# Decoder step on one core: the samples' last store goes out on SyncE instead of GpSimd, and VectorE evicts its rows

## The chip, the cores and the metric

The kernel runs on one core of a Trainium2 chip, as one launch. The metric is the device time of that launch in microseconds. Engines are named as the profile names them: PE (TensorE matmuls), DVE (VectorE), ACT (ScalarE), POOL (GpSimd), SP (SyncE). SP, ACT and POOL can issue DMAs.

## The reference

One step of a hybrid decoder trunk of one layer, for 256 prompt tokens and 8 sample tokens that share the weights (width 2048, f32):

```
h = RMSNorm(x);  q|k|v|z|xBC|dt|qm|gates = h @ w_in
A = sliding-window attention;  B = Mamba-2 SSD;  M = cross-attention into 256 memory tokens
x = x + (sig(gA)*(A @ w_up_swa) + sig(gB)*(B @ w_up_ssd) + sig(gM)*(M @ w_up_mem)) @ w_out
x = x + (silu(h2 @ w_gate) * (h2 @ w_up)) @ w_down        # h2 = RMSNorm(x), d_ff 5632
```

It returns `y_prompt` (1, 256, 2048), `y_sample` (8, 1, 2048) and the new caches and states. What the change touches is the very last piece of the last line: columns 1536 to 2047 of `y_sample`.

## The kernel before

**Layout.** Activations stand transposed: features on the 128 partitions, the 264 tokens (256 prompt, then 8 samples) along the free axis. Each projection is cut into groups of 512 output features, four PSUM tiles of 128 x 264. Weights come in `raw` tiles of 512 KB on SP's queue (L261), are split into a rounded high part (`hi`, ACT, L181) and a rest (`lo`, DVE, L182), and each weight block gives three matmuls (L160).

**The last product.** The FFN runs in three passes over d_ff; in each, `down(i, ...)` for i = 0 to 3 adds 512 features of `@ w_down` to `x2["x"]` in SBUF. In the third pass the sums are outputs. For i = 0 to 2, `y_out` turns tiles by a DVE transpose and stores them from POOL (L1764: a 16 KB store of the samples; L1767: four 128 KB stores of the prompt). For i = 3, `group` is given `bank=y_bank`: it finishes the four PSUM tiles one after the other (c = 0 to 3) and calls `y_bank(ps, c)` after each.

**`y_bank`.** For every c, DVE adds the residual: 8 sample columns (L1777) into `yo_s`, 256 prompt columns (L1779) into `yo`, for c = 3 in two halves. For c = 0 to 2, DVE turns the prompt's columns in 32 x 32 blocks into the buffer `ring` (L1782), and four stores of 32 KB go out, two on SP and two on ACT (L1785). For c = 3 PE turns instead: first `yo_s`, which holds the samples' columns of all four c, into 32 rows of 128 (L1789, written `tr`, shown by the profile as L164, tile `yt`), then the two halves of the prompt's last 128 features. The samples' rows are copied to `ring` and stored (L1790, L1791: 16 KB); the two prompt halves are copied by DVE (t = 0) and ACT (t = 1) and stored by SP and ACT (L1799, L1797, L1800: 64 KB each).

**Order.** A scheduler places each engine's instructions; the order in which the code is written sets their priority. `keep_in_program_order` pins the transposes. Each engine works through its own list in order and waits on semaphores. When the kernel function returns, closing code follows that the profile puts on L1913: each engine's queue is drained, SP waits for the semaphores of the outstanding DMAs, and POOL gathers all engines in a barrier, clears the semaphores and releases them.

Of the kernel before, what the change touches and what calls it, by code (L numbers as in the profile page):

```python
# [12 lines left out]
AF = mybir.ActivationFunctionType  # L13
# [5 lines left out]
P = 128  # L19
# [58 lines left out]
def tile_hybrid_decoder_step(  # L78
# [9 lines left out]
    nc = tc.nc  # L88
    act = nc.scalar.activation
    V = nc.vector  # L90
# [18 lines left out]
    def t4(name, dt=F32):  # L109
        return tp.tile([P, 4 * NT], dt, tag="t4", name=nm(name), bufs=4)  # L110
# [45 lines left out]
    def sps(name):  # L156
        return pq.tile([P, 512], F32, tag="s", name=nm(name))
# [4 lines left out]
    def tr(out, in_):  # L162
        n = in_.shape[0]
        return nc.tensor.transpose(out, in_, ident[0:n, 0:n])  # L164
# [1606 lines left out]
    def y_bank(ps, c):  # L1771

        if c == 0:
            y_end["o"] = t4("yo")
        yo, yo_s = y_end["o"][:, 0:4 * NP].rearrange("p (c n) -> p c n", c=4), y_end["o"][:, 4 * NP:4 * NT]
        x = x2["x"](12 + c)
        V.tensor_tensor(yo_s[:, c * NS:(c + 1) * NS], ps[c][:, NP:NT], x[:, NP:NT], op=ALU.add)  # L1777
        for cols in (slice(0, NP),) if c < 3 else (slice(0, P), slice(P, NP)):
            V.tensor_tensor(yo[:, c, cols], ps[c][:, cols], x[:, cols], op=ALU.add)  # L1779
        if c < 3:  # L1780
            ot = ring[:, c * NP:(c + 1) * NP]
            V.transpose(ot, yo[:, c, 0:NP])  # L1782
            to = y_prompt[0].rearrange("(j t) (k a f) -> k a t j f", t=32, a=4, f=32)[12 + c]
            for a in range(4):
                (nc.sync, nc.scalar)[a % 2].dma_start(to[a], ot[32 * a:32 * a + 32].rearrange("p (j f) -> p j f", f=32))  # L1785
            return
        rows = ring[0:32, 2048 - P:2048]
        ts = sps("yt")
        tc.keep_in_program_order(tr(ts[0:32, 0:P], yo_s))  # L1789
        act(rows, ts[0:32, 0:P], AF.Copy)  # L1790
        nc.gpsimd.dma_start(y_sample.rearrange("b s (k f) -> k (b s) f", f=P)[12:16], rows)  # L1791
        for t in range(2):
            turned = (dps, sps)[t]("yt")
            tc.keep_in_program_order(tr(turned[:, 0:P], yo[:, 3, t * P:(t + 1) * P]))
            ot = ring[:, 1024 + (2 + t) * P:1024 + (3 + t) * P]
            if t:
                act(ot, turned[:, 0:P], AF.Copy)  # L1797
            else:
                V.tensor_copy(ot, turned[:, 0:P])  # L1799
            (nc.scalar if t else nc.sync).dma_start(y_prompt[0, t * P:(t + 1) * P, 15 * P:16 * P], ot)  # L1800
# [116 lines left out]
```

## Time and profile before

| | us |
|---|---|
| median of three runs (1865.42, 1865.45, 1867.88) | 1865.45 |
| the profiled execution, whole | 1866.6 |
| its span, first to last instruction | 1864.9 |
| PE busy in it | 1852.9 |
| DVE / ACT / POOL busy | 1201.3 / 956.2 / 149.6 |

The span lies inside the profiled execution's own time; 1.7 us lie around it. The profile is of one execution, the median of others, so a sum is made against 1866.6 and 1864.9 and then set beside 1865.45. "L1791" is line 1791 of the kernel. "POOLq" or "SPq" are an engine's queue (DMA issues, waits, drains), which are not counted as busy. Instructions of the closing code stand on L1913, those of the opening code on L1904.

### The profile page before, as it was taken

What the parts mean: (1) busy time and instruction counts of PE and PEld (TensorE: products, weight loads), DVE (VectorE), ACT (ScalarE), POOL (GpSimd) and SP (SyncE); (2) the same over time, 40 slices, a digit from 0 to 9 for tenths busy, and PEclk for the clock granted to TensorE, in tenths of its full rate; (3) what the DMA queues carried; (4) which work ended last, traced back from release to release, by engine and by line L of the source; (5) the groups of instructions that cost most, each with busy time, mean ns of one, the idle gap of its engine ahead of it and who ended that gap; (6) DMA issues with size and microseconds to landing.
All of it is one profiled execution on the core that took longest, in us unless ns stands there. A gap on an engine that the chain in (4) does not pass through costs nothing.

```text
span 1864.9 us, 37297 instructions
## 1 busy us (share of the span) xinstructions
PE 1852.9 (99%) x15094; PEld 1811.8 (97%) x15094; DVE 1201.3 (64%) x2329; ACT 956.2 (51%) x1413; POOL 149.6 (8%) x299
## 2 busy tenths in 40 slices
PE   9999999999999999999999999999999999999998
PEld 7899999998999999999999999999999999999998
DVE  6766578776788878887465675555445555445564
ACT  6745466665777676764444444443334443334442
POOL 1010002101111111120000001000000000100001
PEclk9999999999999999999999999999999999999999
DMA  9786669677777777787878766556765556865565
GB/s 308 241 253 213 203 226 303 212 242 237 239 229 263 239 240 245 245 258 236 230 230 252 183 202 213 183 185 179 183 186 183 183 186 185 232 199 181 182 198 132
DMA packets 209669, 406.36 MB, mean 218 GB/s; under 512 B 29319, under 2 KB 34422, under 8 KB 209488
## 3 DMA queue, kind: packets, MB, share of 16 engines
q1 hardware_dynamic: 181552, 324.62, 57.9%
q0 software_dynamic: 21776, 74.10, 11.9%
q10 hardware_dynamic: 6168, 5.25, 0.9%
q8 instruction: 118, 1.93, 0.4%
q14 instruction: 55, 0.45, 0.1%
HBM read 378.38 MB, written 27.81 MB: 218 GB/s over the span
## 4 chain that ended last, share of the span: by engine, by line
PE 60%; issue 1%; DVE 0%; POOL 0%; POOLq 0%; DVEq 0%
PE pg L160 14%; PE pu L160 14%; PE pdn L160 13%; PE pin L160 7%; PE pout L160 5%; PE pus L160 5%; PE pua L160 2%; DVE lo L182 0%; PE py L160 0%; POOL out_dram L1767 0%; PE pst L160 0%; DVE ring L1763 0%; DVE ring L1504 0%; DVE y L1463 0%; DVE xp L1761 0%
## 5 line engine op out<-in xcount | busy, mean ns | idle before, releaser
L182 DVE TENSOR_TENSOR lo<-raw,hi 128x1024 fp32r<-128x1024 f32 (+1 forms) x651 | 746.9, 1152 | 547.8 <-ACT hi L181 545.5
L181 ACT ACTIVATE hi<-raw 128x1024 fp32r<-128x1024 f32 (+1 forms) x651 | 647.6, 1002 | 815.0 <-PE pin L160 188.8
L160 PE MATMUL pin<-hl,hi 128*128 128x264 f32 x1728 | 486.1, 284 | 0.0
L160 PE MATMUL pin<-hh,hi 128*128 128x264 f32 x1728 | 485.5, 284 | 0.0
L160 PE MATMUL pin<-hh,lo 128*128 128x264 f32 x1728 | 474.6, 283 | 0.1
L160 PEld LDWEIGHTS pin<-hl,hi 128*128 128x128 f32 x1728 | 324.2, 188 | 3.7 <-issue 3.6
L160 PEld LDWEIGHTS pin<-hh,hi 128*128 128x128 f32 x1728 | 323.8, 188 | 3.9 <-issue 3.4
L160 PEld LDWEIGHTS pin<-hh,lo 128*128 128x128 f32 x1728 | 318.2, 188 | 3.7 <-issue 3.1
L160 PE MATMUL pu<-h2l,hi 128*128 128x264 f32 x704 | 197.8, 282 | 0.0
L160 PE MATMUL pu<-h2h,hi 128*128 128x264 f32 x704 | 197.7, 282 | 0.0
L160 PE MATMUL pdn<-fal,hi 128*128 128x264 f32 x704 | 197.7, 282 | 0.0
L160 PE MATMUL pg<-h2l,hi 128*128 128x264 f32 x704 | 197.7, 283 | 0.0
L160 PE MATMUL pdn<-fah,hi 128*128 128x264 f32 x704 | 197.3, 282 | 0.0
L160 PE MATMUL pg<-h2h,hi 128*128 128x264 f32 x704 | 197.0, 282 | 0.0
L160 PE MATMUL pdn<-fah,lo 128*128 128x264 f32 x704 | 194.8, 282 | 0.0
L160 PE MATMUL pu<-h2h,lo 128*128 128x264 f32 x704 | 194.7, 282 | 0.0
L160 PE MATMUL pg<-h2h,lo 128*128 128x264 f32 x704 | 194.4, 282 | 0.0
L160 PEld LDWEIGHTS pdn<-fal,hi 128*128 128x128 f32 x704 | 132.0, 188 | 0.0
L160 PEld LDWEIGHTS pg<-h2l,hi 128*128 128x128 f32 x704 | 132.0, 187 | 0.0
L160 PEld LDWEIGHTS pu<-h2l,hi 128*128 128x128 f32 x704 | 132.0, 187 | 0.0
L160 PEld LDWEIGHTS pg<-h2h,hi 128*128 128x128 f32 x704 | 132.0, 187 | 0.0
L160 PEld LDWEIGHTS pu<-h2h,hi 128*128 128x128 f32 x704 | 131.9, 187 | 0.0
(530 smaller groups left out, 2935.3 us busy)
## 6 DMA issues: line engine op xcount, KB each, us to landing
raw<-in_w_in_dram SPq DMA_DIRECT2D x216, 512.0 KB, 4.5
raw<-in_w_gate_dram SPq DMA_DIRECT2D x88, 512.0 KB, 3.6
raw<-in_w_up_dram SPq DMA_DIRECT2D x88, 512.0 KB, 3.9
raw<-in_w_down_dram SPq DMA_DIRECT2D x88, 512.0 KB, 5.0
raw<-in_w_up_ssd_dram SPq DMA_DIRECT2D x32, 512.0 KB, 6.0
raw<-in_w_out_dram SPq DMA_DIRECT2D x32, 512.0 KB, 5.1
raw<-in_w_mem_kv_dram SPq DMA_DIRECT2D x31, 512.0 KB, 5.2
ring<-in_state_ssm_dram POOLq DMA_DIRECT2D x32, 256.0 KB, 5.0
```

The lines of the kernel that those rows point to most:

```text
L160: return nc.tensor.matmul(out, lhsT=lhsT, rhs=rhs, start=start, stop=stop)
L181: h = act(hi, src, AF.Copy)
L182: return h, V.tensor_tensor(lo, src, hi.bitcast(F32), op=ALU.subtract)
```

## The change

The copy of the samples' rows out of PSUM is a DVE `tensor_copy` instead of an ACT activation, and the store is issued on SP's queue instead of POOL's. The rows, their place in `ring` and the destination are the same.

```
         rows = ring[0:32, 2048 - P:2048]
         ts = sps("yt")
         tc.keep_in_program_order(tr(ts[0:32, 0:P], yo_s))
-        act(rows, ts[0:32, 0:P], AF.Copy)
-        nc.gpsimd.dma_start(y_sample.rearrange("b s (k f) -> k (b s) f", f=P)[12:16], rows)
+        V.tensor_copy(rows, ts[0:32, 0:P])
+        nc.sync.dma_start(y_sample.rearrange("b s (k f) -> k (b s) f", f=P)[12:16], rows)
```

Where it puts the two instructions, at the end of three engines' lists (line, operation, output<-input, shape). On DVE, behind the residual adds of c = 3:

```order
 L1777 TENSOR_TENSOR yo_22122<-pdn_22003,x_1710_12828 128x8
 L1779 TENSOR_TENSOR yo_22122<-pdn_22003,x_1710_12828 128x128 x2
+L1790 COPY ring<-yt_22183 32x128
 L1799 COPY ring<-yt_22187 128x128
 L1913 UNCONDITIONAL_BRANCH
```

The copy stands between the last add and the copy of the first prompt half. On SP's queue, behind the last weight load and the six stores of c = 0 to 2:

```order
 L261 DMA raw_22028<-in_w_down_dram 128x2x512
 L1785 DMA out_dram<-ring 32x8x32 x6
+L1791 DMA out_dram<-ring 4x8x128
 L1800 DMA out_dram<-ring 128x128
 L1913 UNCONDITIONAL_BRANCH
```

The samples' store now stands ahead of SP's own last store. On POOL, the end of the list:

```order
 L1764 DMA out_dram<-ys_21982 16x8x32
 L1767 DMA out_dram<-ring 32x8x128 x4
-L1791 DMA out_dram<-ring 4x8x128
 L1913 UNCONDITIONAL_BRANCH
 L1913 ISA
```

POOL's last own work is now the store of the prompt's features of i = 2. On ACT the copy of L1790 is gone from between the six stores of L1785 and the copy of L1797; PE's list is the same.

## The prediction

> **What bounds the kernel now.** The head of the page, read first, says where 99% of the time is.
>
> ```profile
> span 1864.9 us, 37297 instructions
> PE 1852.9 (99%) x15094; PEld 1811.8 (97%) x15094; DVE 1201.3 (64%) x2329; ACT 956.2 (51%) x1413; POOL 149.6 (8%) x299
> ```
>
> PE is busy from end to end; nothing in the change touches a matmul that lies ahead of the last store, so the body of the program stays as it is. All that can move lies behind the last projection matmul. The second view is therefore the chain that ended last, from 1835 us on; its last five pieces are:
>
> ```profile
> 1841.82 1.39 POOL out_dram L1767 x3
> 1843.21 0.33 issue
> 1843.54 0.58 POOL out_dram L1767
> 1844.12 14.28 issue
> 1858.40 0.63 POOLq L1913
> ```
>
> The chain ends on POOL's own queue, in the closing code (L1913), not on PE, SP or ACT. The 14.28 us of "issue" are POOL waiting for the sample's rows. The third view, the timeline from 1852 us on without the weight loads, shows what is done there; columns are start, duration, engine, line, operation.
>
> ```profile
> 1853.67 3.71 SPq L1785 DMA_DIRECT2D out_dram<-ring  x6
> 1853.67 3.78 ACTq L1785 DMA_DIRECT2D out_dram<-ring  x6
> ...
> 1856.70 0.28 PE L160 MATMUL pdn<-fah,lo 128*128 128x264 f32 x1
> 1857.10 0.48 DVE L1779 TENSOR_TENSOR yo<-pdn,x 128x128 f32<-128x128 f32 x2
> 1857.24 0.73 PE L164 MATMUL yt<-ident,yo 128*32 128x128 f32 x3 [0.26 <-DVE yo L1777]
> 1857.81 0.29 DVE L1799 COPY ring<-yt 128x128 f32<-128x128 f32 x1 [0.23 <-PE yt L164]
> 1857.87 0.27 ACT L1790 ACTIVATE ring<-yt 32x128 f32<-32x128 f32 x1 [8.59 <-PE yt L164]
> 1858.04 0.27 ACT L1797 ACTIVATE ring<-yt 128x128 f32<-128x128 f32 x1
> 1858.13 0.36 SPq L1800 DMA_DIRECT2D out_dram<-ring  x1
> 1858.34 0.37 ACTq L1800 DMA_DIRECT2D out_dram<-ring  x1
> 1858.42 0.61 POOL L1791 DMA_DIRECT2D out_dram<-ring  x1 [14.30 <-ACT ring L1797]
> ```
>
> The last matmul ends at 1856.98, the three last stores are issued within 0.3 us of each other (1858.13, 1858.34, 1858.42), and the last descriptor work that the timeline shows ends at 1859.03. The span still goes on to 1864.9. The fourth view, the closing code's own instructions on POOL and SP, shows with what (columns: count, then shortest/median/longest in ns, then first and last start). The L1904 row is POOL's drain at the program's head, and the last two rows are POOL's over the whole close.
>
> ```profile
> L1913 POOLq DRAIN  x1: 5692/5692/5692, 1858.4 to 1858.4; - x1
> ...
> L1913 SPq EVENT_SEMAPHORE  x9: 28/28/1814, 1858.5 to 1860.8; - x9
> L1913 SPq DRAIN  x2: 7/7/7, 1860.9 to 1860.9; - x2
> ...
> L1904 POOLq DRAIN  x1: 183/183/183, 0.4 to 0.4; - x1
> ...
> L1913 POOLq EVENT_SEMAPHORE  x4: 17/17/17, 1864.1 to 1864.8; - x4
> L1913 POOLq DRAIN  x3: 46/108/5692, 1858.4 to 1864.6; - x3
> ```
>
> The reader is to see two clocks running side by side. SP waits for the transfers: its first closing wait takes 1.81 us (1858.53 to 1860.34), eight more follow in a row until 1860.8, and its drains stand at 1860.9; then it has nothing left. POOL's first closing drain starts with the store's issue at 1858.40 and takes 5.69 us, to 1864.09; POOL's next closing instruction starts at 1864.1 and the span ends 0.8 us later. So SP waits some 3.2 us for POOL. The waits of SP's queue say the same:
>
> ```profile
> SPq L1913 <- PEq L1913: 3.8, 2, 3.4
> SPq L1913 <- DMA out_dram<-ring: 1.8, 1, 1.8
> ```
>
> The 3.4 us (put down to PE's queue, which had drained long before) is the gap between SP's end and POOL's. It is what this change can win or miss.
>
> **The change, part by part.** One store leaves POOL for SP, one 32x128 copy leaves ACT for DVE. PE's order is the same.
>
> *POOL loses the store of L1791* (0.61 us of descriptor work) and with it the reason for a late drain. POOL's last work is then the L1767 store that ends at 1844.12. Its closing drain can start there. What a drain costs behind a store is shown once only, 5.69 us from dispatch, of which 5.06 us lie behind the end of the store's descriptor work (1859.03 to 1864.09); drains with no store just ahead took 0.183, 0.108 and 0.046 us. With the long value it ends near 1849.2, with the short ones at 1844.2; both are covered by PE, which works until 1856.98. If the drain grew for the burst of five stores there, it would have 16 us of cover before it reached SP's end. I cost it at nothing.
>
> *DVE gains the copy of L1790.* The rows of the three transposes and of the nearest copy of that shape on DVE:
>
> ```profile
> L164 PE MATMUL yt<-ident,yo x3: 284/329/331, 1857.2 to 1857.6; 128*128 128x128 f32 x2, 128*32 128x128 f32 x1
> ...
> L1343 DVE COPY par<-pr 32x128 f32<-32x128 f32 x1 | 0.2, 216 | 0.0
> ```
>
> It needs the first of the three transposes (from 1857.24, 0.28 us by the row above: 1857.52) and DVE free of the adds (1857.10 + 0.48 = 1857.58). It runs from 1857.58 to some 1857.80, at the longer L1799 duration to 1857.87. L1799 waits for the second transpose and starts at 1857.81 now; behind the new copy it starts between 1857.81 and 1857.87. Lower bound 0, upper bound 0.07 us; I take 0.03, and SP is later than that anyway.
>
> *ACT loses the copy of L1790.* L1797 behind it needs the third transpose (1857.24 + 0.73 = 1857.97) and starts at 1858.04 now, so at most 0.07 us can be won. What could be lost: L1790, the first copy after 8.59 us of idle, started 0.35 us after its transpose ended at 1857.52; if L1797 inherits that lag it starts at 1858.32, 0.28 later. I take no change, because ACT's six stores end at 1853.67 + 3.78 = 1857.45 and leave it free well before 1857.97, and put ACT's store at 1858.34, between 1858.27 and 1858.62.
>
> *SP gains the store of L1791, ahead of its own L1800.* Issue and landing of SP's stores of this stage, and the landing of the moved store on POOL's queue, are:
>
> ```profile
> L1785 SPq DMA_DIRECT2D out_dram<-ring x6: 315/372/450, 1853.7 to 1857.0; - x6
> DMA to landing us min/median/max: 1.6/1.8/1.8
> ...
> L1800 SPq EVENT_SEMAPHORE  x2: 28/28/28, 1857.4 to 1857.5; - x2
> ...
> DMA to landing us min/median/max: 1.9/1.9/1.9
> ```
>
> (The first landing row is that of L1785's stores, the second that of L1791's.) SP's six L1785 stores end at 1853.67 + 3.71 = 1857.38, so SP is free. The new store is issued at about 1857.85, takes 0.36 us, and the two semaphore instructions that L1800 needs and that ran ahead of time before now stand behind it, some 0.06 us each with the gap between them. L1800 goes out at 1858.33 instead of 1858.13: 0.2 us later, between 0.1 (everything at its shortest) and 0.4 (0.45 us of issue and the long copy). That is the cost of one queue for two stores.
>
> The Trainium skill, page "DMA: Bandwidth & Descriptors", section "Issuing engines are not separate DMA queues", speaks against the change here: all queues share the same 16 DMA engines, and starting DMAs from several engines saves the issue time on the sequencer. By that rule alone the moved store would only add SP's issue time, those 0.2 us, and bring nothing.
>
> *Landing.* The first wait of SP now ends at 1860.34, which fits POOL's store (1858.42 + 1.9). The 64 KB stores of L1800 show no landing of their own; the eight waits behind the first go through at 0.06 us each, so they had landed by then: at most 1860.34 - 1858.13 = 2.2 us. From below the smaller stores' 1.6 us. I take 1.8, the row that is nearest in queue and kind. SP's L1800 then lands at 1858.33 + 1.8 = 1860.13, ACT's at 1860.14, the sample's at 1859.65: all a little earlier than the 1860.3 of POOL's slower queue. Bounds 1859.9 and 1860.6.
>
> *SP's remaining waits.* Nine waits stand in a row. Those on long finished transfers that come ahead of the last landing cost nothing, those behind it 0.06 us each: 0 to 0.5 us. I take 0.25. With the drains (0.1), SP is through at 1860.13 + 0.25 + 0.1 = 1860.5, against 1860.95 now; bounds 1860.1 and 1861.1 (late landing with all eight waits behind it would be 1861.2, which I count as an edge).
>
> *The close.* From POOL's first closing semaphore instruction (1864.1) to the end of the span are 0.75 to 0.8 us of barrier, clear and barrier. None of it depends on the store. End of the span: 1860.55 + 0.8 = 1861.35, against 1864.9.
>
> **Sum.** Gain 3.55 us by this account; between 2.9 (all late) and 3.9 (all early). The profiled execution took 1866.6 us, of which 1864.9 are span; the rest, 1.7 us, stays. It would become 1863.05. The median of the runs without a profile is 1865.45, 1.15 lower than the profiled one. Taking the same difference off gives 1861.9; as the late side of three terms is wider than the early side I take 1862.0. What can be told from no change is 0.2%, 3.73 us, that is 1861.72. The forecast is thus a real gain that lies just under that bound.
>
> **The rivals.**
>
> *The drain's length hangs on the end of the program, not on POOL's own last store.* If POOL's drain waits for every transfer of the core and then needs its 3.75 us (1860.34 to 1864.09), moving the store changes nothing but the landing: -0.2 to +0.3 us, so 1865.5. For it: only one long drain is in the trace, so store and program end can't be told apart. Against it: the drain starts with POOL's own store and no other engine's drain lasts; SP's take 7 ns. The Trainium skill, page "VectorE: DVE Perf Modes", section "The DRAIN you can't avoid", says that the drains of the opening and closing code are about 12 ns, constant, on all engines. By that rule POOL's store could not be what stretches a drain, and this rival would hold; the row of 5692 ns on POOL disagrees with it, SP's 7 ns agree.
>
> *Slower: the drain pays for each store in POOL's last burst.* There are five of them, behind which POOL now goes to its drain at once:
>
> ```profile
> 1840.61 0.53 POOL L1764 DMA_DIRECT2D out_dram<-ys  x1 [13.26 <-DVE ys L1762]
> 1841.82 2.30 POOL L1767 DMA_DIRECT2D out_dram<-ring  x4 [0.68 <-DVE ring L1763]
> ```
>  At 5.06 us each the drain would end at 1844.12 + 25.3 = 1869.4 and the span at 1870.2: 1870.8 us for the kernel, 5.3 us slower. It decides from (1864.1 - 1844.1) / 5 = 4.0 us per store. Against it: the four L1767 stores take 2.30 us, 0.58 us each, so the engine isn't held 5 us by each. For it: no drain behind more than one store is in the trace.
>
> *Late side of the forecast: SP becomes the bound and loses more than I give it.* Two stores on SP, ACT's copy 0.28 late, landing at 2.0 and all eight waits behind it: 1861.2 for SP, 1862.0 for the span, a gain of 2.9: 1862.55.
>
> *Early side.* ACT's copy wins its 0.07, landings of 1.7, the waits on the two stores come last of the nine: SP through at 1860.2, span 1861.0, a gain of 3.85: 1861.6. That is faster by over 0.2%.
>
> **How the numbers follow.** Forecast (gain between 3.0 and 3.73) 0.45; early side 0.30; late side 0.13; drain tied to the program's end 0.08; drain paid per store 0.04. Within 0.2%: 0.45 + 0.13 + most of the 0.08, 0.64 in all. Faster: 0.31, nearly all of it the early side. Slower: the 0.04 and a remainder, 0.05. The forecast's own range is 1861.7 to 1862.5. The stated range takes in the early side (gains up to 4.3, since the three runs before differ by 2.5 us among themselves) and the late side with a margin for the same reason: 1861.1 to 1863.4. The two drain rivals, 0.12 together, are left out with some of the tails.
>
> **What would show it.** Right: POOL's closing drain starts at about 1844 and ends by 1850; the chain that ends last runs over SP's or ACT's store, its landing and SP's closing waits; SP's closing drain is followed within 0.1 us by POOL's semaphore instruction; the store of L1791 stands on SP's queue 0.4 to 0.5 us ahead of L1800, which starts 0.1 to 0.4 us later than 1858.13; L1799 starts within 0.07 us of where it was; everything before 1856.98 is the same. Wrong: a long POOL drain that starts or ends behind 1858, a landing over 2.2 us, or ACT's store later than 1858.62.

## The result and the profile after

| | before | after |
|---|---|---|
| median of 13 runs each, us | 1866.02 (1865.22 to 1868.18) | 1862.57 (1861.68 to 1864.62) |
| ratio | | 0.9981 [0.9973, 0.9988] |
| the profiled execution / its span, us | 1866.6 / 1864.9 | 1862.84 / 1861.1 |

The change gains 3.45 us by the medians. The forecast was 1862.0 against a median of 1865.45, a gain of 3.45 too; the median of before came out 0.57 higher this time. The gain lies at the bound of what can be told from no change (0.2%), and its interval excludes 1.

The head of the page of the changed kernel:

```profile
span 1861.1 us, 37297 instructions
PE 1853.6 (100%) x15094; PEld 1813.0 (97%) x15094; DVE 1201.8 (65%) x2330; ACT 956.7 (51%) x1412; POOL 149.4 (8%) x298
```

PE is no faster (1853.6 against 1852.9); one instruction went from ACT to DVE, one left POOL. The chain that ended last, of the changed kernel from 1835 us on (start, duration, what):

```profile
1834.91 21.60 PE pdn L160 x179
1856.51 0.02 issue
1856.53 0.18 DVE yo L1777
1856.71 0.04 issue
1856.75 0.74 PE yt L164 x3
1857.49 0.02 issue
1857.51 0.28 ACT ring L1797
```

Where before it ran from the L1767 stores through 14 us of POOL's idleness into POOL's drain, it now runs over PE, the last residual add, the transposes and ACT's last copy. It stops there, at 1857.79, though the span goes on to 1861.1: what follows are transfers and waits. The timeline of the changed kernel around the last stores (start, duration, engine, line, operation):

```profile
1856.53 0.17 DVE L1777 TENSOR_TENSOR yo<-pdn,x 128x8 f32<-128x8 f32 x1 [0.48 <-PE pdn L160]
...
1857.08 0.28 DVE L1790 COPY ring<-yt 32x128 f32<-32x128 f32 x1
...
1857.32 0.29 DVE L1799 COPY ring<-yt 128x128 f32<-128x128 f32 x1
1857.38 0.75 SPq L1791 DMA_DIRECT2D out_dram<-ring  x1
1857.51 0.28 ACT L1797 ACTIVATE ring<-yt 128x128 f32<-128x128 f32 x1 [8.72 <-PE yt L164]
1857.82 0.37 ACTq L1800 DMA_DIRECT2D out_dram<-ring  x1
1858.32 0.37 SPq L1800 DMA_DIRECT2D out_dram<-ring  x1
```

The closing code of the changed kernel on POOL's and SP's queues (count, shortest/median/longest in ns, first and last start):

```profile
L1913 POOLq DRAIN  x1: 5925/5925/5925, 1842.7 to 1842.7; - x1
...
L1913 SPq EVENT_SEMAPHORE  x11: 17/28/28, 1858.7 to 1861.0; - x11
L1913 SPq DRAIN  x3: 7/7/7, 1860.3 to 1860.6; - x3
...
L1913 POOLq EVENT_SEMAPHORE  x4: 17/17/17, 1860.3 to 1861.0; - x4
```

POOL's first closing drain is about as long as before (5.93 us against 5.69), but it starts at 1842.70 and ends at 1848.62. That is 11.7 us ahead of SP's second closing drain at 1860.31, SP's last instruction ahead of the barrier, which POOL's next instruction follows in the same tenth. The barrier no longer waits for POOL but for SP. The waits of SP's queue (in all, times, longest) say it too: the 3.4 us put down to PE's queue have become 0.5, and what is left are transfers.

```profile
SPq L1913 <- DMA out_dram<-ring: 1.0, 3, 0.5
SPq L1913 <- PEq L1913: 0.7, 2, 0.5
```

Two executions differ by some tenths in when PE's body ends. To take that out, the last residual add of the samples (L1777 for c = 3, first line of the timeline above) serves as a zero point. Before it started here:

```profile
1857.02 0.17 DVE L1777 TENSOR_TENSOR yo<-pdn,x 128x8 f32<-128x8 f32 x1 [0.47 <-PE pdn L160]
```

From there to the end of the span, it is 7.87 us before and 4.56 after; this stretch is called the tail from here on. So of the 3.8 us by which the spans differ, 3.31 come from the tail, and 0.49 from an earlier end of the body, which the change doesn't touch. The tails of all large kernels are below, with SP's second closing drain and the end of POOL's first closing drain, all in us after the start of that add, from the events of one profiled execution of each.

| kernel | median, ratio [95%] | SP's drain | POOL's drain ends | tail |
|---|---|---|---|---|
| before | 1866.02 | 3.91 | 7.08 | 7.87 |
| after | 1862.57, 0.9981 [0.9973, 0.9988] | 3.78 | -7.91 | 4.56 |
| e1 store alone | 1863.00, 0.9984 [0.9975, 0.9993] | 4.02 | -7.92 | 4.80 |
| e2 copy alone | 1865.73, 0.9997 [0.9988, 1.0006] | 3.97 | 6.79 | 7.58 |
| e4 store on ACT | 1862.72, 0.9982 [0.9973, 0.9991] | 4.01 | -7.91 | 4.79 |
| e3 late POOL copy | 1864.75, 0.9993 [0.9984, 1.0001] | 3.82 | 6.11 | 6.91 |
| e6 c = 0 store on POOL | 1862.63, 0.9982 [0.9973, 0.9991] | 3.86 | 2.56 | 4.64 |
| e7 c = 2 store on POOL | 1864.26, 0.9991 [0.9981, 1.0] | 3.87 | 5.46 | 6.25 |
| e5 late copy, drain at 7.5 us | 1864.79, 0.9994 [0.9985, 1.0003] | 3.78 | 6.10 | 6.91 |
| e9 late copy, drain ahead | 1862.63, 0.9982 [0.9972, 0.9991] | 3.78 | 1.19 | 4.55 |

The table can be read by one rule: the tail is the later of the two middle columns plus 0.77 to 0.80 us for the barrier and the end. A negative value lies ahead of the add. The rows of each kernel stand with the experiments.

### The profile page after: what moved, and what is told of

Its sections match the earlier page's. It is cut to its first block, busy times and chain, and to the rows that moved or that the text cites. A ratio compares the mean times of both kernels' runs of the same rounds, so it can differ in the third digit from the quotient of the medians.

```text
span 1861.1 us, 37297 instructions
## 1 busy us (share of the span) xinstructions
PE 1853.6 (100%) x15094; PEld 1813.0 (97%) x15094; DVE 1201.8 (65%) x2330; ACT 956.7 (51%) x1412; POOL 149.4 (8%) x298
## 3 DMA queue, kind: packets, MB, share of 16 engines
q10 hardware_dynamic: 6168, 5.25, 0.9%
## 4 chain that ended last, share of the span: by engine, by line
PE 61%; DVE 1%; ACT 0%; issue 0%
PE pdn L160 14%; PE pg L160 14%; PE pu L160 14%; PE pin L160 7%; PE pout L160 5%; PE pus L160 5%; PE pua L160 3%; DVE lo L182 0%; PE py L160 0%; DVE ring L1504 0%; ACT dec L1408 0%; PE pst L160 0%; ACT ring L1503 0%; DVE y L1463 0%; DVE jkh L1505 0%
```

## The experiments

Edits are shown against the changed kernel. The question of the first three is which half of the change brings the gain; of the next three, what makes POOL's drain long and when it shows; of the rest, what the length hangs on. Each kernel was compared with runs of before on its own chip (medians 1866.01 to 1866.09).

**The store alone (e1).** The copy stays on ACT:

```
-        V.tensor_copy(rows, ts[0:32, 0:P])
+        act(rows, ts[0:32, 0:P], AF.Copy)
```

> Only the store moves to SP; the copy of the samples' rows stays on ACT. On SP the store then stands behind L1800, not ahead of it. Drain theory (the gain is POOL's long drain leaving the end): nearly the whole gain, 3.1 to 3.6 us, ratio 0.9981 to 0.9984; POOL's long drain near 1842 to 1849; the last landing is the samples' store, issued near 1858.0 with an issue of 0.75 us. Rival (the copy on DVE, which is ready some 0.3 us sooner and takes a step off ACT, brings it): under 0.7 us, ratio over 0.9996.

Measured: 1863.00 us, 0.9984 [0.9975, 0.9993]. The rows of its POOL drain and of its last copies and stores on the timeline:

```profile
L1913 POOLq DRAIN  x1: 5918/5918/5918, 1842.3 to 1842.3; - x1
```

```profile
1857.00 0.27 ACT L1790 ACTIVATE ring<-yt 32x128 f32<-32x128 f32 x1 [8.59 <-PE yt L164]
...
1857.26 0.36 SPq L1800 DMA_DIRECT2D out_dram<-ring  x1
...
1857.78 0.75 SPq L1791 DMA_DIRECT2D out_dram<-ring  x1
```

The store alone brings nearly all: the tail is 4.80 against 4.56. With the copy on ACT the scheduler also turned the two stores of SP round: L1800 goes first and the samples' store follows, so the last issue ends 2.38 us after the start of that add (1858.53 against 1856.15), on the changed kernel 2.16 us after it. So what the copy on DVE adds, with the order of the two stores that comes with it, is about 0.2 us of tail, less than the runs can tell apart (1863.00 against 1862.57 with overlapping intervals).

**The copy alone (e2).** The store goes back to POOL:

```
-        nc.sync.dma_start(y_sample.rearrange("b s (k f) -> k (b s) f", f=P)[12:16], rows)
+        nc.gpsimd.dma_start(y_sample.rearrange("b s (k f) -> k (b s) f", f=P)[12:16], rows)
```

> Only the copy moves to DVE; the store stays on POOL. Drain theory: the rows are ready about 0.3 us sooner, POOL's store is issued 0.2 to 0.5 us sooner, its drain still takes 5.6 to 5.7 us from there and ends last: gain 0.2 to 0.5 us, ratio 0.9997 to 0.9999. Rival (the copy on DVE brings the gain): 2.5 us or more, ratio 0.9987 or less.

Measured: 1865.73 us, 0.9997 [0.9988, 1.0006]: no difference. POOL's store on the timeline, and POOL's drain behind it:

```profile
1857.93 0.61 POOL L1791 DMA_DIRECT2D out_dram<-ring  x1 [14.00 <-DVE ring L1799]
```

```profile
L1913 POOLq DRAIN  x1: 5695/5695/5695, 1857.9 to 1857.9; - x1
```

The drain ends 5.06 us behind the store's descriptor work, which is the time that POOL is busy with a DMA instruction (1863.60 against 1858.54). That is the lag of before. Moving the copy moves POOL's store 0.3 us forward against that add (tail 7.58 against 7.87) and no more.

**The store on ACT's queue (e4).** This asks if it matters that it is SP:

```
-        nc.sync.dma_start(y_sample.rearrange("b s (k f) -> k (b s) f", f=P)[12:16], rows)
+        nc.scalar.dma_start(y_sample.rearrange("b s (k f) -> k (b s) f", f=P)[12:16], rows)
```

> The changed kernel with the samples' store on ACT's queue instead of SP's. Drain theory: any queue but POOL's does; what is lost is ACT's own end: the store's issue of 0.75 us stands ahead of ACT's last copy and store, which go out 0.6 to 0.9 us later, while SP's last store goes out 0.6 us sooner. Gain 2.6 to 3.2 us, ratio 0.9983 to 0.9986, POOL's drain over by 1850. Rival (SP's queue is what matters, for instance since SP makes the closing waits): a gain under 1.5 us.

Measured: 1862.72 us, 0.9982 [0.9973, 0.9991], which can't be told from after; the gain, 3.4 us, is a little over the 2.6 to 3.2 that were expected. The three last stores on its timeline:

```profile
1856.87 0.66 ACTq L1791 DMA_DIRECT2D out_dram<-ring  x1
...
1857.11 0.36 SPq L1800 DMA_DIRECT2D out_dram<-ring  x1
...
1858.03 0.37 ACTq L1800 DMA_DIRECT2D out_dram<-ring  x1
```

Here SP's own store goes out early and ACT's is the late one; its tail is 4.79. What counts is that the store isn't on POOL. The Trainium skill, page "DMA: Bandwidth & Descriptors", section "Issuing engines are not separate DMA queues", says that starting DMAs on several engines saves only the time that it takes to initiate them. These runs show one more difference: POOL was busy for 0.61 us with the store and SP's issue took 0.75, yet the kernel with the store alone moved to SP (e1) is 3.1 us faster than before.

**A late copy on POOL instead of the store (e3).** The prediction put the long drain down to the store. Here POOL gets a small copy inside SBUF at the same place, and no DMA:

```
         V.tensor_copy(rows, ts[0:32, 0:P])
+        nc.gpsimd.tensor_copy(tiny("late", 64)[0:32], rows[:, 0:64])
```

> The changed kernel, with one more instruction on POOL that is no DMA: a copy of 32x64 of the samples' rows inside SBUF, as late as the store was. Its output is used by nobody. Theory that the long drain is what follows a store issued by POOL: the store of L1767 is over 10 us old by then, the drain behind the copy takes 0.1 to 0.5 us, the time is that of the changed kernel (ratio 0.9981, within 0.0005). Rival that the drain costs 5 us whenever it comes late or behind any work of POOL: it ends near 1857.7 + 5 = 1862.7, 2.4 us behind SP, ratio near 0.9993.

Measured: 1864.75 us, 0.9993 [0.9984, 1.0001]. The copy on the timeline, then the closing code on POOL and SP:

```profile
1857.46 0.23 POOL L1790 COPY late<-ring 32x64 f32<-32x64 f32 x1 [13.78 <-DVE ring L1790]
```

```profile
L1913 POOLq DRAIN  x1: 5243/5243/5243, 1857.4 to 1857.4; - x1
...
L1913 SPq DRAIN  x3: 7/7/7, 1860.3 to 1862.9; - x3
...
L1913 POOLq EVENT_SEMAPHORE  x4: 17/17/17, 1862.7 to 1863.4; - x4
```

A copy of 0.23 us costs 2.35 us of tail (6.91 against 4.56), since the drain behind it is nearly as long: it ends 4.99 us behind the copy's end. The cause as the prediction named it, a drain behind a *store*, is too narrow. In this kernel the drain is long behind both kinds of late POOL work that were tried, a store and a copy.

**A store of c = 0, then of c = 2, on POOL (e6, e7).** These two vary how late POOL's last work is: one of the 32 KB stores of L1785 goes from SP to POOL, at two distances from the end. The first edit is shown; the second has (2, 2).

```
-        (nc.sync, nc.scalar)[a % 2]
+        (nc.gpsimd if (c, a) == (0, 2) else (nc.sync, nc.scalar)[a % 2])
```

> The changed kernel with one 32 KB store of c = 0 (L1785, one of four) issued by POOL. If 5.0 us follow POOL's last work wherever it lies: that store's descriptor work ends 6.3 us ahead of SP's closing drain (about 1853.9 against 1860.3), the drain ends 1.4 us ahead of SP: no cost, ratio 0.9981 (within 0.0005). Rival (any POOL work in the last stage costs the time back): ratio over 0.9988.

> The same with one store of c = 2 on POOL. Its descriptor work ends near 1856.8, the drain near 1861.8, 1.4 us behind SP: POOL ends last again and the span is 1.2 to 1.6 us longer than that of the changed kernel, ratio 0.9987 to 0.9990. Rival (only the very last store matters): 0.9981.

Measured: 1862.63 us, 0.9982 [0.9973, 0.9991], with the early store; 1864.26, 0.9991 [0.9981, 1.0], with the late one. The closing code with the early store:

```profile
L1913 POOLq DRAIN  x1: 5662/5662/5662, 1853.0 to 1853.0; - x1
...
L1913 SPq DRAIN  x3: 7/7/7, 1859.9 to 1860.2; - x3
...
L1913 POOLq EVENT_SEMAPHORE  x4: 17/17/17, 1860.0 to 1860.7; - x4
```

And with the late one:

```profile
L1913 POOLq DRAIN  x1: 5665/5665/5665, 1856.2 to 1856.2; - x1
...
L1913 SPq DRAIN  x3: 7/7/7, 1860.2 to 1862.1; - x3
...
L1913 POOLq EVENT_SEMAPHORE  x4: 17/17/17, 1861.9 to 1862.6; - x4
```

Both drains are 5.66 us long. The first ends at 1858.69, 1.3 us ahead of SP's drain, and costs nothing; the second ends at 1861.87, 1.6 us behind it, and the tail grows by 1.70 us (1.2 to 1.6 were expected). This is the plain arithmetic of two clocks and it also shows that the drain doesn't wait for the end of the program: with the early store it is over before the last stores have landed.

**A drain ahead of the late copy (e5, e9).** If the 5 us are a debt that gathers with POOL's DMAs and is settled once, a drain written earlier, under PE's work, should take it, and the late copy should then be free. The first try put a bare drain where the code of `y_bank` begins c = 0:

```
-            y_end["o"] = t4("yo")
+            y_end["o"] = t4("yo"); nc.gpsimd.drain()
...
         V.tensor_copy(rows, ts[0:32, 0:P])
+        nc.gpsimd.tensor_copy(tiny("late", 64)[0:32], rows[:, 0:64])
```

> The kernel with the late POOL copy, plus one drain of POOL written into the program behind its L1767 stores. The late copy alone cost the 5 us again, so the store itself is not what is paid for. Theory A (a debt that POOL's DMAs leave, paid by the first drain, for instance of their queue): the written drain takes 5.0 us behind the stores and the closing drain behind the copy under 0.5 us; ratio 0.9981. Theory B (every drain behind POOL work so far down the program costs 5 us): the closing drain is 5.2 us again, ratio 0.9993 as with the late copy alone.

Measured: 1864.79 us, 0.9994 [0.9985, 1.0003], like e3. The two drains of POOL:

```profile
L1774 POOLq DRAIN  x1: 4062/4062/4062, 7.5 to 7.5; - x1
```

```profile
L1913 POOLq DRAIN  x1: 5240/5240/5240, 1856.9 to 1856.9; - x1
```

This run doesn't decide. The drain depends on nothing, and the scheduler moved it to 7.5 us, behind POOL's first 8 DMAs; the other 230 came after it. It took 4.06 us there, but six of the 8 DMAs had not landed when it began, and it ended 0.37 us behind the last landing (11.56 against 11.19, from the trace's events). So it may have waited for these transfers, and its length says nothing of DMAs that are done. The second try holds it in place, in written order behind the L1767 stores and ahead of the late copy:

```
-            nc.gpsimd.dma_start(to[a], ...)                                  # L1767
+            tc.keep_in_program_order(nc.gpsimd.dma_start(to[a], ...))
...
+            if c == 0: tc.keep_in_program_order(nc.gpsimd.drain())           # end of the branch c < 3
...
         V.tensor_copy(rows, ts[0:32, 0:P])
+        tc.keep_in_program_order(nc.gpsimd.tensor_copy(tiny("late", 64)[0:32], rows[:, 0:64]))
```

> The kernel with the late POOL copy and a drain of POOL that is held in place behind the L1767 stores (the drain written in before had moved to 7.5 us and lay ahead of nearly all of POOL's DMAs, so it did not decide). Theory A (a debt that POOL's DMAs leave and the first drain behind them pays): the written drain takes 4.9 to 5.1 us behind the last L1767 store, hidden by PE; the closing drain behind the late copy under 0.5 us; ratio 0.9981 to 0.9984. Theory B (in this program every drain that follows POOL work costs it): the closing drain 5.2 us, ratio 0.9993.

Measured: 1862.63 us, 0.9982 [0.9972, 0.9991]: the cost of the late copy is gone. The written drain, the late copy on the timeline, and the closing code (L1914 here, since one line was added):

```profile
L1786 POOLq DRAIN  x1: 5920/5920/5920, 1842.5 to 1842.5; - x1
```

```profile
1857.19 0.23 POOL L1791 COPY late<-ring 32x64 f32<-32x64 f32 x1 [13.78 <-DVE ring L1791]
```

```profile
L1914 POOLq DRAIN  x1: 320/320/320, 1857.2 to 1857.2; - x1
...
L1914 SPq DRAIN  x3: 7/7/7, 1860.0 to 1860.3; - x3
```

The same copy at the same place is followed by a drain of 0.320 us instead of 5.243; it ends 0.07 us behind the copy. The 5 us were paid at 1842.5, under PE's work. So they belong to something that POOL's earlier work leaves behind and that the first drain settles, once.

**What leaves it behind (e8, e12, e10, e11).** Four small programs leave out nearly all of the computation: they load rows, add, store, and end with the same 32x64 copy on POOL. Only their closing drain is read, in one execution of each; their whole times say nothing here. They differ in POOL's earlier work: memsets alone; memsets and an identity matrix; one DMA of 1 MB; 64 DMAs of 64 KB.

```
 e8   nc.sync.dma_start(w, x_prompt[0, 0:P])
 e12  nc.sync.dma_start(w, x_prompt[0, 0:P]);  make_identity(nc, ident)      # on POOL
 e10  nc.gpsimd.dma_start(w, x_prompt[0, 0:P])
 e11  for k in range(64): nc.gpsimd.dma_start(w[:, ...], x_prompt[0, 0:P, ...])
```

> The closing drain by itself: a program of a few instructions that loads x_prompt's first 128 rows, adds them up ten times on DVE and stores, and leaves all else of the computation out. POOL issues no DMA; behind the adds it copies 32x64 in SBUF. Theory A (a debt of POOL's DMAs): the closing drain takes 0.1 to 0.3 us. Theory B: about 5 us.

> The same program without a POOL DMA, but with the identity matrix built on POOL, whose selecting instruction brings POOL's configuration change with it, as the large kernel has. If POOL's DMAs make the drain long: 0.3 us as without. If the configuration change does: 3.5 us or more.

> The program of a few instructions again (it leaves most of the computation out), now with one 1 MB load issued by POOL at its start, over 20 us ahead of the late copy. Without a POOL DMA its closing drain took 0.32 us, 0.07 us behind the copy. If one DMA is enough to make the drain long: 3.5 us or more. If the length goes with the number of DMAs: under 0.5 us.

> The same with 64 loads of 64 KB issued by POOL. If the drain is long as soon as there was any DMA of POOL: the same length as with one, 3.5 to 5.3 us. If it goes with the number (238 DMAs: 5.0 us): 1.2 to 1.6 us.

POOL's three closing drains of each (the longest value is the first of them), in that order; the third and fourth with the row of their POOL DMAs from the groups by line (count, busy us, mean ns), the fourth also with its copy on the timeline:

```profile
L139 POOLq DRAIN  x3: 34/70/316, 31.1 to 35.6; - x3
```

```profile
L141 POOLq DRAIN  x3: 34/70/314, 30.4 to 34.9; - x3
```

```profile
L99 POOL DMA_DIRECT2D w<-in_x_prompt_dram x1 | 0.7, 652 | 0.4 <-issue 0.4
```

```profile
L139 POOLq DRAIN  x3: 34/82/410, 31.0 to 35.4; - x3
```

```profile
L100 POOL DMA_DIRECT2D w<-in_x_prompt_dram x64 | 33.8, 537 | 0.4 <-issue 0.4
```

```profile
61.36 0.23 POOL L107 COPY late<-acc 32x64 f32<-32x64 f32 x1 [26.31 <-DVE acc L104]
```

```profile
L140 POOLq DRAIN  x3: 40/95/5561, 61.3 to 67.4; - x3
```

Behind the end of the copy, the drain lasts 0.07 us without DMAs, 0.07 with the identity, 0.16 with one DMA, 5.31 with 64. In all four the loads had long landed when the copy began, since the copy reads what was added up from them; the last of the 64 landed at 36.68, 24.7 us ahead of the copy. So it is POOL's own DMAs that make the first drain long, though they are done. Neither theory holds as it was put: one DMA isn't enough for a long drain, and 64 don't give the 1.2 to 1.6 us that a length in proportion to 238 would. From one DMA to 64 there is a step or a slope that these runs don't resolve. One DMA adds 0.09 us to the drain and 64 add 5.25, so an estimate of 0.08 to 0.09 us for each, up to a limit, fits too, but isn't shown. From 64 to the large kernel's 238 it grows no more (5.31 against 5.0 to 5.1). One DMA of 1 MB and 64 of 64 KB also differ in bytes (4 MB in all) and in descriptors, and the runs don't separate these from the count.

## Why the prediction was right, and where it was not

**Right: where the gain is.** That PE's body stays, that SP waits for POOL's drain alone, that this drain can run under PE's work once POOL has nothing late, and that the close behind the later of the two takes some 0.8 us: each stands in the rows above. The time, 1862.57, lies in the stated range. It is 0.07 above the likeliest case's own (1861.7 to 1862.5), with a median of before that was itself 0.57 higher. The gain is as forecast, and that it is so to the hundredth is luck, as the terms below show.

**Right: the little weight given to the two rivals about the drain.** "It hangs on the end of the program" fails on the changed kernel itself (the drain ends at 1848.62) and on e6. "It is paid per store" fails too: behind the five stores it ends 4.98 us after the last one's descriptor work (1843.65 to 1848.62), as it did behind one (5.06). The Trainium skill, page "VectorE: DVE Perf Modes", section "The DRAIN you can't avoid", whose rule was weighed in the prediction, says some 12 ns for such drains on all engines; POOL's 5925 ns disagree with it, SP's 7 ns are near it. Where POOL had no DMA to settle, the trace comes nearer to it (0.32 us in e9, of which 0.07 lie behind POOL's work), but not to 12 ns.

**Too narrow: the mechanism.** The step "POOL loses the store and with it the reason for a late drain" names the store as the reason. The one long drain of before couldn't tell a store from any late work, and the prediction chose the nearer reading. E3 shows that a late copy does it too, and e9 and the small programs that the 5 us are left by POOL's DMAs before and settled by the first drain behind them. For this change both readings give the same time; for a kernel in which a late POOL copy remains they would not.

**Mis-sized: SP's issue of the moved store.** "Takes 0.36 us" is what L1800 took on the same queue, near the 0.37 of the L1785 stores there. It took 0.754:

```profile
L1791 SPq DMA_DIRECT2D out_dram<-ring x1: 754/754/754, 1857.4 to 1857.4; - x1
```

On ACT's queue it took 0.66 (e4). A row of before with a like destination was there and wasn't used: the stores of L1323, which go out in short runs too, on ACT's queue.

```profile
L1323 ACTq DMA_DIRECT2D acs_d<-acsT x2: 602/892/1181, 459.0 to 460.2; - x2
```

So SP's L1800 started 1.79 us after the start of the samples' last add, against 1.11 before: 0.68 later, where the prediction took 0.2 and allowed 0.4. The sign that it gave of being right, 0.1 to 0.4 us later, did not come. That the shape of the destination sets the issue time fits both rows but wasn't tried by itself, and the two stores of L1323 differ by a factor of two among themselves.

**Paid back in part by the other terms.** SP's store landed in 1.67 us (1858.32 to 1859.99, from the trace's events), faster than the 1.8 taken; ACT's took 1.94, the samples' 2.02. From that landing to SP's second drain it took 0.32 us, where 0.35 was taken, and from there to the end 0.78, where the account gave 0.85 (its 0.8, and 0.05 by which 1860.5 became 1860.55 without a term for it). L1799 wasn't delayed (0.79 us after the start of that add in both), and ACT's L1797 did not inherit the lag of 0.35: its copy starts 0.02 us behind the transposes, and ACT's store goes out 1.29 us after the start of the add, against 1.32. SP was then through 0.14 us earlier than before where 0.45 was forecast; the tail gained 3.31 us where the account had 3.55. The medians show 3.45, 0.14 more than the tail, where runs of one kernel differ by up to 3 us. That the forecast said 3.45 too, with 0.1 taken off its account beforehand, is a coincidence. The allowance "as the late side is wider" was for the right side, but SP's issue went beyond its own late bound.

**Not tried.** The store on POOL with a drain written ahead of it was not run. By e9 the drain behind it should be short, but there POOL's late work was a copy and not another DMA. None of e1, e4, e6 and e9 can be told from the changed kernel; no version better than it was found.

## What to carry to other kernels

Look at the closing code before tuning the last microseconds: if POOL has issued many DMAs in the program (64 and 238 here), its first drain ends some 5 us behind its last work, even behind a copy of 0.2 us, and shows in the time whenever that work lies less than about 5 us ahead of the end of SP's waits. Take POOL's last work off the end, move it some 5 us earlier, or write a drain, pinned in order, where another engine's work covers it (shown here for a late copy). And when you price a moved DMA, look also for rows with its destination's shape, not only for the row nearest in size or queue.

## What the runs showed of the hardware that was not expected

- A drain on POOL's queue is long once and then short: 5.92 us behind 238 DMAs that had all but the last few long landed, 0.32 us behind work that issued no further DMA (e9). Without POOL DMAs it is 0.31 to 0.32 us, with one 0.41, with 64 5.56.
- The length hardly depends on what came last: the drain ends 5.06 us behind a store (before, e2, e6, e7), 4.98 behind five (after), 4.99 behind a copy (e3).
- A 16 KB store with a 4x8x128 destination took 0.75 us of SP's queue and 0.66 of ACT's (e4); a 64 KB store of 128x128 took 0.37 on both.
